# Gate projection in a decoder layer: five seven-product pairs between plain tiles, weight splits tied behind their place, and token sums over twelve steps

## The chip, the cores and the metric

The kernel runs on one core of one Trainium2 chip. The metric is the device time of one execution in microseconds; a run of the kernel before has a median of 2108.14 us over three runs (2105.8 to 2109.37).

Five engines work from their own queues: TensorE (PE in the profile, its weight loads PEld), VectorE (DVE), ScalarE (ACT), GpSimd (POOL) and SyncE (SP), which here issues the DMAs.

## What the kernel computes

One layer of a decoder on 1024 tokens of width 1024, in float32: a half-step SwiGLU, a mixing block, a half-step SwiGLU. The change lies in the mixing block. Its core in the reference:

```python
h = rms_norm(x, mix_norm)
q_lat, kv_lat, k_rope, fq, fk, fv, f_logit, g_mla, g_fox = split(h @ w_in)
y_mla = mla_mixer(...)   # 8 heads, causal softmax attention, 128-query blocks
y_fox = fox_mixer(...)   # 8 heads, the same with a cumulative log-forget-gate bias
mixed = (sigmoid(g_mla + b_gate[0]) * (y_mla @ w_branch_mla)
         + sigmoid(g_fox + b_gate[1]) * (y_fox @ w_branch_fox))
x = x + mixed @ w_o
```

`g_mla` and `g_fox` are each 1024 tokens by 1024 columns: the *gate projection*, `h` times 2048 columns of `w_in`. It needs nothing of the attention, and the attention needs nothing of it until the branches are mixed.

## The kernel before

**Products.** Every large product is made of float16 pairs: an operand is split into a high half (ScalarE: scale and cast, L167) and a low half (VectorE: scaled operand minus the high half, L170), both in `split_sb` (L161), and three matmuls (high-high, high-low, low-high) stand for one. A weight tile that comes by DMA goes through this split before TensorE can use it.

**Two ways to do the gate projection.** A *plain tile* (`gate_steps`, L1718) takes 128 columns: `col_load` brings them into a `stg` buffer, `col_split` makes `whi` and `wlo`, and each half of the tokens (512) takes 24 matmuls of 128x512 in two steps of 12. A *pair* (`gate_pairs`, L1753) takes 256 columns: the weight block and the token block are each cut in four quarters, and seven products of quarter sums give what eight products of quarters would (Strassen's scheme in Winograd's form). Each of the seven products is 12 matmuls and one step, so a pair takes 84 matmuls in 7 steps where two plain tiles take 96 in 8. For that it needs sums of the weight quarters and of the token quarters.

**Weight sums.** `operands` (L1062) makes them on GpSimd and is a Python generator. The sums `s3`, `a21+a22` and `s2` (L1068, L1069, L1070) come when a pair is begun; a fourth, the entry "-" of the order string, is `a12-s2` (L1075) and overwrites `a12`. Every further `next` splits one of the seven operands. The order is "12 11 - s2 s3 22 21 12": the first "12" is the untouched quarter, the last one the sum. `begin` (L1761) issues the load of a pair's weights into an `act` slot, `sums` (L1770) calls the generator for the three sums and the splits of "12" and "11", and `step` (L1780) does one product and draws the next operand. In steps q = 0 to 4 it draws one each: the "-" with `s2` in q = 0, then `s3`, 22, 21 and the last 12. At q = 4 the next pair's load is begun, at q = 6 its sums.

**Token sums.** `token_sums` (L889) forms four sums of token quarters on VectorE (L919 to L930), each in two halves, and splits them (high on ScalarE, L909; low on VectorE, L913): eight times a sum, a high and a low.

**The attention loop.** `attention` (L1847) runs 64 steps: 16 heads (8 MLA, then 8 FoX) of 4 steps, each step two 128-query blocks. A step does the scores of its two blocks (L1984), the row maximum on VectorE (`nm`, L1988), the exponential on ScalarE (L1991); then, one step late, the transposes of the probabilities on TensorE (L2010), their split (L167, L170), the product with the values (`pspv`, L2020 and L2025) and its combination (`cmb`: ScalarE L2027, VectorE L2028, GpSimd L2030 to L2032). After a pair of heads, `rest` (L2056) scales the result on GpSimd. Between these, gate steps are popped from a list so that TensorE has other matmuls while it waits for a softmax: 53 steps, about one a loop step, are dealt out over steps 0 to 53. Five plain steps are popped before the loop, 11 follow in steps 0 to 10, and the pairs come after them. The list `jobs` puts the parts of the forget-gate chain (`forget`, L1485) ahead of steps 0, 3, 5 and 6, the token sums ahead of steps 1 to 8 (a sum, a high and a low each), the first pair's load ahead of step 8 and its sums ahead of step 10. Near the end of the gate list, four `pieces` load and split the MLA attention result (`sta`, L2105) for the branch product, which starts at step 56.

**What sets the order.** The program is traced in this order, but a scheduler then sets each engine's queue by its own estimate of when an instruction becomes ready, so that an instruction can be placed ahead of others that were traced before it. On the chip each engine takes its queue in that fixed order. `follow(name)` (L147) adds an edge without a semaphore: the last traced instruction is placed behind the named one. `latest(engine)` (L191) is the last traced instruction of an engine. The splits of the weight sums have no such edge before the change.

**Buffers.** Tiles of one tag share a fixed number of slots: 8 of `u`, 4 each of `v`, `act` and `wd`. During the loop four `u` slots hold the split tokens and two the token sums; two `act` slots hold probabilities, one the values, and one is left for the weights of a pair.

Of the kernel before, what the change touches and what calls it, by code (L numbers as in the profile page):

```python
# [13 lines left out]
F16 = mybir.dt.float16  # L14
# [38 lines left out]
class Parts:  # L53
# [5 lines left out]
    def at(self, k, s=slice(None)):  # L59
        return self.tiles[k // self.per][:, k % self.per, s]  # L60
# [5 lines left out]
class Layer:  # L66
# [197 lines left out]
    def layer(self):  # L264
        src = self.i["x"][0]
# [49 lines left out]
        gates = []  # L315
        self.in_proj(hT, gates, lat["mark"])
        first = self.attention(gates, mix)
        ws = []
# [743 lines left out]
    def operands(self, w, scale, tags, order):  # L1062
# [10 lines left out]
        for name in order.split():  # L1073
            if name == "-":
                pool(out=a12, in0=a12, in1=s2, op=ALU.subtract)  # L1075
                self.behind = self.latest(mybir.EngineType.Pool)
                continue
            if tags is None:
                tag = ("stg", "whi", "wlo", "atp")[self.opn % 4]
                self.opn += 1  # L1080
            else:
                tag = next(tags)
            o = self.ring.tile([P, 2, 4, P], F16, tag=tag, bufs=2, name="op")
            self.split_sb(o[:, 0], o[:, 1], src[name], scale)
            yield o[:, 0], o[:, 1]
# [632 lines left out]
    def gate_steps(self, hT):  # L1718
# [3 lines left out]

        order = [(0, d, n) for d in range(4) for n in range(2)]
        weights = {}

        def prep(i):
            if i >= len(order):
                return
            s, d, n = order[i]
# [7 lines left out]
        def step(i, q):  # L1737
            s, d, n = order[i]
            if q == 0:
                self.gps = self.psb("psgate") if i % 2 and i < 2 else self.psg("psgate")  # L1740
                prep(i + 1)
            self.proj_half(self.gps, weights[i], hT, n, range(4 * q, 4 * q + 4))
# [6 lines left out]

        prep(0)  # L1750
        return [lambda a=(i, q): step(*a) for i in range(len(order)) for q in range(2)]

    def gate_pairs(self, every):  # L1753

        nc = self.nc
        w_in = self.i["w_in"][0]
        pairs = [(0, 4), (0, 6), (1, 0), (1, 2), (1, 4), (1, 6)]
        box = {"ops": []}
# [21 lines left out]
        def step(p, q):  # L1780
# [4 lines left out]
            e = box["e"]  # L1785
# [4 lines left out]
            self.product(ps, box["ops"].pop(0), every((1, 0, 3, 5, 6, 2, 4)[q]), first)  # L1790
            if q < 5:
                box["ops"].append(next(box["gen"]))

# [23 lines left out]
    def branch_mla_steps(self):  # L1817
# [4 lines left out]
        def piece(p):  # L1822
            if p == 0:
                box["at"] = [self.parts(tag, 4, 4, F16, 4096) for tag in ("u", "act")]
            self.split_at(box["at"], 0, p)
# [20 lines left out]

    def attention(self, gates, mix):  # L1847

# [27 lines left out]
        sum_of, high, low, every = self.token_sums(mix)  # L1876
        begin, sums, steps = self.gate_pairs(every)
        gates += steps
        total = len(gates)
        chain = self.forget()  # L1880
        jobs = {}
        at = lambda i, f: jobs.setdefault(i, []).append(f)
        for i in (0, 3, 5, 6):
            at(i, lambda: next(chain, None))
        for n, (k, e) in enumerate((k, e) for k in (3, 1, 2, 4) for e in range(2)):
            for f in (sum_of, high, low):
                at(n + 1, lambda f=f, k=k, e=e: f(k, e))
        at(8, lambda: begin(0))
        at(10, lambda: sums(0))
        for i in range(2 * HEADS * GR):  # L1890
# [18 lines left out]
            pr.append(self.scores(ops[k], 2 * g + 1, j, rs, pbuf))  # L1909
            if i <= 55:  # L1910
                while gates and done < total * (i + 1) / 55:
                    gates.pop(0)()
                    done += 1
                if len(gates) <= 3 and pieces:
                    pieces.pop(0)()
# [309 lines left out]
```

## Time and profile before

| | |
|---|---|
| median of 3 runs | 2108.14 us |
| the profiled execution | 2108.31 us, span of its instructions 2106.5 us |
| TensorE busy | 2040.2 us, 97% of the span |
| VectorE, ScalarE, GpSimd busy | 71%, 57%, 34% |
| attention with the gate steps, about 862 to 1335 us | TensorE busy 433.71 of 473 us, granted clock 0.96 |
| granted clock over the span | 0.989 |

All times in the profile are counted from the first instruction. A row of a group reads: line, engine, operation, tile written and tiles read, shape, count, then busy time and the mean of one in ns, then the engine's idle time just before such instructions and what ended it. In a table by stretches, each engine has its busy time and the count of instructions, and then come the granted TensorE clock (1.00 is full), the DMA engines' busy share and GB/s. A busy TensorE at a clock of 0.5 does half the work.

### The profile page before, as it was taken

Reading aid. Unit: us, or ns where it says so; the run is one execution under the profiler, and the core shown is the slowest. Engines: PE = TensorE matmul, PEld = TensorE weight load, DVE = VectorE, ACT = ScalarE, POOL = GpSimd, SP = SyncE. Lnnn points to the kernel's source line nnn. Section 1 sums busy time; section 2 is a strip of 40 time slices with the busy share of each in tenths; the row PEclk is TensorE's granted clock in tenths of the full one; section 3 lists DMA queues with packets and bytes.
Section 4 is the critical chain, followed back from the end, with each engine's and each line's share of the span. In section 5 each row is a group of like instructions: output and inputs, shape, how many; then the busy total and the mean of one; then the engine's idle time right before and its main releaser. Section 6 shows DMA issues by size and latency. Waiting matters only on the chain.

```text
span 2106.5 us, 28666 instructions
## 1 busy us (share of the span) xinstructions
PE 2040.2 (97%) x10175; PEld 1110.7 (53%) x10175; DVE 1504.6 (71%) x2515; ACT 1192.2 (57%) x2013; POOL 708.4 (34%) x759
## 2 busy tenths in 40 slices
PE   8999999999999999999998989999999999999999
PEld 5444444444447555466665655468544444444445
DVE  7856666788888788598777876864675555559876
ACT  6666665545555454477676765422556666555552
POOL 4455544752202121123332322000155554564300
PEclk9999999999999999999999999999999999999999
DMA  8258675675444564644454575452454464356433
GB/s 226 75 156 266 208 235 183 222 265 172 134 140 149 170 171 138 188 115 116 115 145 129 138 194 146 154 169 79 120 147 144 138 204 123 131 191 224 140 104 116
DMA packets 271546, 336.01 MB, mean 160 GB/s; under 512 B 21785, under 2 KB 201865, under 8 KB 271402
## 3 DMA queue, kind: packets, MB, share of 16 engines
q1 hardware_dynamic: 271402, 334.18, 52.1%
q8 instruction: 80, 1.31, 0.3%
q14 instruction: 64, 0.52, 0.1%
HBM read 240.32 MB, written 93.81 MB: 159 GB/s over the span
## 4 chain that ended last, share of the span: by engine, by line
PE 76%; DVE 11%; ACT 4%; DMA 3%; issue 3%; POOL 1%; SPq 1%; ACTq 0%; DVEq 0%; POOLq 0%
PE pst L1094 19%; PE psd L1247 15%; PE psb L1094 11%; PE psgate L1094 3%; PE psg L1094 3%; PE pspt L2010 3%; PE pss L1984 3%; DVE op L170 2%; PE pspv L2020 2%; PE psb L159 2%; PE psb L157 2%; PE psb L158 2%; PE psin L159 1%; PE psin L157 1%; PE psin L158 1%
## 5 line engine op out<-in xcount | busy, mean ns | idle before, releaser
L1094 PEld LDWEIGHTS <-op 128*128 128x128 f16 x3864 | 374.4, 98 | 439.9 <-issue 6.7
L1247 PE MATMUL psd<-op 128*128 128x512 f16 x1680 | 364.3, 379 | 1.8 <-DVE op L170 1.7
L1247 PEld LDWEIGHTS <-op 128*128 128x128 f16 x1680 | 164.3, 98 | 200.6 <-issue 3.5
L170 DVE SCALAR_TENSOR_TENSOR op<-s_u,s_v,op 128x512 f16<-128x512 f32 x170 | 151.0, 898 | 89.4 <-ACT op L167 88.8
L1094 PE MATMUL pst<-s_u,op 128*128 128x512 f16 x720 | 165.2, 379 | 1.3 <-DVE s_act L1142 1.3
L1094 PE MATMUL pst<-s_v,op 128*128 128x512 f16 x720 | 165.2, 379 | 1.3 <-DVE s_u L1142 1.3
L167 ACT ACTIVATE op<-s_u,s_v 128x512 f16<-128x512 f32 x170 | 118.0, 715 | 83.8 <-PE psd L1247 71.5
L170 DVE SCALAR_TENSOR_TENSOR op<-s_act,s_wd,op 128x512 f16<-128x512 f32 x130 | 117.8, 919 | 59.0 <-ACT op L167 59.0
L2010 PE MATMUL pspt<-ident,s_act 128*128 128x128 f32 x576 | 97.2, 290 | 30.7 <-ACT s_act L1991 17.5
L1991 ACT ACTIVATE s_act<-pss,nm 128x128 f32<-128x128 f32 (+7 forms) x128 | 94.4, 738 | 56.5 <-DVE nm L1988 55.6
L1984 PE MATMUL pss<-s_wd 96*128 96x256 f32 (+5 forms) x480 | 123.7, 381 | 0.7 <-DMA s_wd<-mk 0.6
L2030 POOL COPY atp<-cmb 64x128 f32<-64x128 f32 x64 | 24.3, 379 | 290.0 <-DVE cmb L2028 290.0
L1068 POOL TENSOR_TENSOR sums<-s_u 128x512 f32<-128x512 f32 x20 | 25.8, 1289 | 255.4 <-PE psa L615 160.9
L170 DVE SCALAR_TENSOR_TENSOR s_v<-pspt,s_v 128x512 f16<-128x512 f32 (+1 forms) x160 | 96.0, 630 | 13.8 <-ACT s_v L167 12.8
L2010 PEld LDWEIGHTS pspt<-ident,s_act 128*128 128x128 f32 x576 | 69.3, 147 | 61.3 <-ACT s_act L1991 34.1
L167 ACT ACTIVATE s_v<-pspt 128x512 f16<-128x512 f32 (+1 forms) x160 | 82.5, 552 | 24.9 <-PE pspt L2010 22.2
L1988 DVE TENSOR_REDUCE nm<-pss 128x1 f32<-128x128 f32 (+7 forms) x128 | 94.5, 750 | 1.6
L167 ACT ACTIVATE op<-s_wd 128x512 f16<-128x512 f32 x70 | 50.4, 721 | 78.6 <-PE psd L1247 74.9
L167 ACT ACTIVATE op<-s_act,s_wd 128x512 f16<-128x512 f32 x130 | 88.8, 710 | 6.6 <-PE pst L1094 4.1
L1094 PE MATMUL psgate<-s_u,op 128*128 128x512 f16 x360 | 87.8, 382 | 0.0
L1984 PEld LDWEIGHTS pss<-s_wd 96*128 96x128 f32 (+1 forms) x480 | 82.5, 201 | 8.9 <-ACT s_act L1991 0.9
L1094 PE MATMUL psb<-s_wd,op 128*128 128x512 f16 x360 | 82.6, 379 | 0.0
(566 smaller groups left out, 4575.0 us busy)
## 6 DMA issues: line engine op xcount, KB each, us to landing
sumd<-s_u SPq DMA_DIRECT2D x20, 1024.0 KB
s_u<-in_w_in_dram SPq DMA_DIRECT2D x19, 1024.0 KB
s_wd<-in_ffn_w_down_dram SPq DMA_DIRECT2D x32, 512.0 KB
sumd<-s_wd SPq DMA_DIRECT2D x13, 1024.0 KB
s_wd<-fd SPq DMA_DIRECT2D x48, 256.0 KB
s_act<-in_ffn_w_down_dram SPq DMA_DIRECT2D x22, 512.0 KB
s_wd<-sumd SPq DMA_DIRECT2D x14, 768.0 KB
s_u<-sumd SPq DMA_DIRECT2D x14, 768.0 KB
```

What stands on the lines that cost most here:

```text
L157: mm(out, lhsT=lh, rhs=rh, start=start, stop=False)
L158: mm(out, lhsT=lh, rhs=rl, start=False, stop=False)
L159: mm(out, lhsT=ll, rhs=rh, start=False, stop=stop)
L167: self.nc.scalar.activation(hi, src, AF.Copy, scale=scale)
L170: self.nc.vector.scalar_tensor_tensor(out=lo, in0=src, scalar=scale, in1=hi, op0=ALU.mult, op1=ALU.subtract)
L1094: mm(out, lhsT=a[:, k, :], rhs=b[:, k, :], start=start and k == 0 and i == 0, stop=k == n - 1 and i == 2, skip_group_check=True,)
L1247: nc.tensor.matmul(o, lhsT=u[:, r], rhs=w, start=start and m == 0, stop=k == CK - 1 and m == 2, skip_group_check=True,)
L1984: mm(ps[:, b:e], lhsT=a[:, q], rhs=bb[:, b:e], start=k == 0, stop=k == len(passes) - 1)
L1988: nc.vector.tensor_reduce(out=nm, in_=ps[:, :n], op=ALU.max, axis=AX.X, negate=True)
L1991: nc.scalar.activation(pn[:, :n], ps[:, :n], AF.Exp, bias=nm, accum_out=rs[:, i, j:j + 1])
L2010: nc.tensor.transpose(pt[:, o:o + P], pr[m][:, kt * P:(kt + 1) * P], self.ident)
L2020: mm(po[:, :256], lhsT=v[:, kt, :], rhs=slab[:, s, c, e * 256:(e + 1) * 256], start=kt == 0 and s == 0, stop=False,)
```

## The change

Plain tiles take six of the sixteen column blocks instead of four: (1, 0) and (1, 1) are added, so there are five pairs, without (1, 0). The order in the loop is 15 plain steps, 35 steps of pairs, then the last 4 plain steps, whose weights are loaded and split by a separate call (`behind`) in the last pair's step q = 5.

The operand generator now returns after the "-" too, and the pair's steps draw (1, 1, 2, 1, 1, 0, 0) times: the "-" alone at q = 0, `s2` at q = 1, `s3` and 22 at q = 2, 21 at q = 3, the last 12 at q = 4. Each split of a pair's operand is tied: its ScalarE half behind ScalarE's latest traced instruction, its VectorE half behind VectorE's.

The token sums, highs and lows are a list of 24, taken two a step in steps 1 to 12, after the step's scores instead of ahead of the step; highs and lows are tied as the splits are. The first pair's load comes in step 11 and its sums in step 13. The forget chain's parts move to steps 2, 4, 6 and 8. Both halves of the MLA branch operand lie in `u` slots, and the `pieces` start with four gate steps left instead of three.

```diff
@@ operands
             if name == "-":
                 pool(out=a12, in0=a12, in1=s2, op=ALU.subtract)
                 self.behind = self.latest(mybir.EngineType.Pool)
+                if tags is not None:
+                    yield None
                 continue
...
-            self.split_sb(o[:, 0], o[:, 1], src[name], scale)
+            last = ()
+            if tags is not None:
+                last = self.latest(mybir.EngineType.Activation), self.latest(mybir.EngineType.DVE)
+            self.split_sb(o[:, 0], o[:, 1], src[name], scale, last)
             yield o[:, 0], o[:, 1]
@@ gate_steps
-        order = [(0, d, n) for d in range(4) for n in range(2)]
+        order = [(s, d, n) for s, d in ((0, 0), (0, 1), (0, 2), (0, 3), (1, 0), (1, 1)) for n in range(2)]
...
-                prep(i + 1)
+                if i + 1 not in (10, 12):
+                    prep(i + 1)
...
-        return [lambda a=(i, q): step(*a) for i in range(len(order)) for q in range(2)]
+        return [lambda a=(i, q): step(*a) for i in range(len(order)) for q in range(2)], lambda: prep(10)
@@ gate_pairs
-        pairs = [(0, 4), (0, 6), (1, 0), (1, 2), (1, 4), (1, 6)]
+        pairs = [(0, 4), (0, 6), (1, 2), (1, 4), (1, 6)]
...
-            if q < 5:
-                box["ops"].append(next(box["gen"]))
+            for _ in range((1, 1, 2, 1, 1, 0, 0)[q]):
+                o = next(box["gen"])
+                if o is not None:
+                    box["ops"].append(o)
+            if (p, q) == (len(pairs) - 1, 5):
+                behind()
@@ branch_mla_steps
-                box["at"] = [self.parts(tag, 4, 4, F16, 4096) for tag in ("u", "act")]
+                box["at"] = [self.parts(tag, 4, 4, F16, 4096) for tag in ("u", "u")]
@@ attention
-        gates += steps
+        gates[15:15] = steps
...
-        for i in (0, 3, 5, 6):
+        for i in (2, 4, 6, 8):
             at(i, lambda: next(chain, None))
-        for n, (k, e) in enumerate((k, e) for k in (3, 1, 2, 4) for e in range(2)):
-            for f in (sum_of, high, low):
-                at(n + 1, lambda f=f, k=k, e=e: f(k, e))
-        at(8, lambda: begin(0))
-        at(10, lambda: sums(0))
+        pinned = []
+        for k, e in ((k, e) for k in (3, 1, 2, 4) for e in range(2)):
+            for f, engine in ((sum_of, None), (high, mybir.EngineType.Activation), (low, mybir.EngineType.DVE)):
+                pinned.append((engine, lambda f=f, k=k, e=e: f(k, e)))
...
             if i <= 55:
+                for engine, f in pinned[2 * i - 2:2 * i] if i else ():
+                    last = engine and self.latest(engine)
+                    f()
+                    if last:
+                        self.follow(last)
+                if i == 11:
+                    begin(0)
+                if i == 13:
+                    sums(0)
...
-                if len(gates) <= 3 and pieces:
+                if len(gates) <= 4 and pieces:
```

More of the change, by code (lines that the diff above doesn't have):

```diff
@@ L316, in layer @@
         self.in_proj(hT, gates, lat["mark"])
-        first = self.attention(gates, mix)
+        first = self.attention(*gates, mix)
         ws = []
@@ L1721, in gate_steps @@
         w_in = self.i["w_in"][0]
-        order = [(0, d, n) for d in range(4) for n in range(2)]
+        order = [(s, d, n) for s, d in ((0, 0), (0, 1), (0, 2), (0, 3), (1, 0), (1, 1)) for n in range(2)]
         weights = {}
         def prep(i):
-            if i >= len(order):
-                return
             s, d, n = order[i]
@@ L1750, in gate_steps, with gate_pairs @@
         prep(0)
-        return [lambda a=(i, q): step(*a) for i in range(len(order)) for q in range(2)]
-    def gate_pairs(self, every):
+        return [lambda a=(i, q): step(*a) for i in range(len(order)) for q in range(2)], lambda: prep(10)
+    def gate_pairs(self, every, behind):
         nc = self.nc
         w_in = self.i["w_in"][0]
-        pairs = [(0, 4), (0, 6), (1, 0), (1, 2), (1, 4), (1, 6)]
+        pairs = [(0, 4), (0, 6), (1, 2), (1, 4), (1, 6)]
         box = {"ops": []}
@@ L1844, in branch_mla_steps, with attention @@
         return pieces, lambda: prep(0), gates, [lambda last=False, a=(d, n): step(*a, last) for d in range(KD) for n in range(2)]
-    def attention(self, gates, mix):
+    def attention(self, gates, more, mix):
         nc = self.nc
@@ L1876, in attention @@
         sum_of, high, low, every = self.token_sums(mix)
-        begin, sums, steps = self.gate_pairs(every)
-        gates += steps
+        begin, sums, steps = self.gate_pairs(every, more)
+        gates[15:15] = steps
         total = len(gates)
```

## The prediction

> **What bounds the kernel now.** I read the page first, then the waits of the stretch in which the gate pairs run, then the timelines around its holes, then a table by stretches.
>
> ```profile
> span 2106.5 us, 28666 instructions
> PE 2040.2 (97%) x10175; PEld 1110.7 (53%) x10175; DVE 1504.6 (71%) x2515; ACT 1192.2 (57%) x2013; POOL 708.4 (34%) x759
> ...
> PE 76%; DVE 11%; ACT 4%; DMA 3%; issue 3%; POOL 1%; SPq 1%; ACTq 0%; DVEq 0%; POOLq 0%
> ```
>
> TensorE is busy for 97% of the span and carries 76% of the chain that ended last. So only two things count: matmuls added or removed, and holes of TensorE, with the slow clock that follows a hole. The profiled execution took 2108.31 us, 1.8 more than its span and 0.17 more than the median of 2108.14; I work from 2108.3.
>
> The waits between 950 and 1250 us, TensorE's first, then two of ScalarE's:
>
> ```profile
> PE pspt L2010 <- DVE cmb L2028: 10.8, 6, 4.0
> PE pspt L2010 <- ACT s_act L1991: 9.3, 10, 3.3
> ```
>
> ```profile
> ACT op L167 <- POOL sums L1070: 13.1, 5, 4.0
> ACT op L167 <- POOL sums L1068: 2.4, 1, 2.4
> ```
>
> (us in total, times, longest.) TensorE waits for softmax results, 20.1 us in all. ScalarE, which makes them, stands 15.5 us in front of a weight-sum split whose sum GpSimd has not finished. Both come together around 1183 us, on ScalarE, then GpSimd, then TensorE:
>
> ```profile
> 1185.10 0.72 ACT L167 ACTIVATE op<-sums,ws 128x512 f16<-128x512 f32 x1 [4.01 <-POOL sums L1070]
> 1185.85 0.58 ACT L2027 COPY cmb<-pspv 64x512 f32<-64x512 f32 x1
> 1186.45 1.11 ACT L1991 ACTIVATE s_act<-pss,nm 128x1024 f32<-128x1024 f32 x1
> ```
>
> ```profile
> 1180.80 1.26 POOL L1068 TENSOR_TENSOR sums<-s_act 128x512 f32<-128x512 f32 x1
> ...
> 1183.81 1.26 POOL L1070 TENSOR_TENSOR sums<-s_act 128x512 f32<-128x512 f32 x1
> ```
>
> ```profile
> 1187.27 0.33 PE L2010 MATMUL pspt<-ident,s_act 128*128 128x128 f32 x1 [4.04 <-DVE cmb L2028]
> ```
>
> ScalarE is idle for 4.01 us until the third sum ends (1183.81 + 1.26 = 1185.07). Behind the blocked split stand the `cmb` copy and an exponential, and TensorE, out of other work, is idle for 4.04 us. The split was put into the queue too early: the scheduler thought the sum would be there.
>
> The table by stretches gives the size of each hole. After its length, a row's first figure is TensorE's busy time; the granted clock stands third from the end.
>
> ```profile
> 886.00:894.00 8.00, 6.02 (x18) 3.53 (x17) 3.28 (x9) 4.56 (x11) 1.13 (x6) 0.59 0.88 206
> 919.00:953.00 34.00, 31.43 (x189) 20.30 (x188) 32.69 (x52) 24.38 (x48) 10.94 (x15) 1.00 0.50 123
> 956.00:968.00 12.00, 8.97 (x53) 5.83 (x51) 11.80 (x15) 7.17 (x13) 6.71 (x7) 1.00 0.46 135
> 1004.00:1010.00 6.00, 5.04 (x31) 3.50 (x29) 5.08 (x9) 4.48 (x10) 3.07 (x4) 1.00 0.78 220
> 1040.00:1050.00 10.00, 8.26 (x39) 6.01 (x38) 6.75 (x10) 7.01 (x13) 3.52 (x5) 0.83 0.04 4
> 1050.00:1116.00 66.00, 65.32 (x406) 44.58 (x405) 50.16 (x95) 49.66 (x102) 20.35 (x37) 1.00 0.60 156
> 1120.00:1132.00 12.00, 9.47 (x60) 5.95 (x58) 9.58 (x15) 8.55 (x18) 3.28 (x7) 1.00 0.82 211
> 1142.00:1156.00 14.00, 10.70 (x47) 6.94 (x46) 9.33 (x16) 7.34 (x13) 6.68 (x8) 0.76 0.18 57
> 1182.00:1194.00 12.00, 7.96 (x46) 5.76 (x44) 6.87 (x13) 6.57 (x13) 5.98 (x7) 0.86 0.60 146
> 1236.00:1246.00 10.00, 7.74 (x50) 4.88 (x49) 7.19 (x14) 6.74 (x14) 1.75 (x5) 1.00 0.95 204
> 1250.00:1282.00 32.00, 22.48 (x115) 16.77 (x113) 23.32 (x40) 19.42 (x40) 5.12 (x14) 0.79 0.80 232
> ```
>
> Five of these stretches (956, 1004, 1040, 1142 and 1182) hold a pair's sums on GpSimd. Their idle time of TensorE is 3.03 + 0.96 + 1.74 + 3.30 + 4.04 = 13.07 us. The one pair left of the six has its sums inside 1050:1116, where none of ScalarE's splits had to wait long for them: 0.68 us of idle in 66 us.
>
> **The change part by part.**
>
> *Splits behind GpSimd and tied.* `s2` was drawn in the step after its pair's sums; now the step after that, and no split may be placed ahead of its traced place. From 962.6 to 1247.2 us there are 42 products:
>
> ```profile
> L1094 PE MATMUL psgate<-s_u,op x360: 376/379/634, 962.6 to 1247.2; 128*128 128x512 f16 x180
> ```
>
> That is 6.8 us a step, so a split two steps behind the sums has some 13 us, and GpSimd's chain took 4.3 us above (1180.80 to 1185.07). The five holes should close. With them goes the slow clock: (1 - 0.83) x 10 + (1 - 0.76) x 14 + (1 - 0.86) x 12 = 6.7 us; some of a hole may itself lie in a slow stretch, so I count 5.7. Together 18.8 us. Bounds: nothing if other waits refill the holes, 19.8 if all goes. Since that one pair was free of it already and showed almost no idle time, I take 85%: -16.0.
>
> [...]
>
> *Five pairs instead of six.* Two plain tiles take 8 steps, a pair 7, so one step of 12 matmuls is added. The chain shows such a step back to back:
>
> ```profile
> 983.12 2.61 PE psgate L1094 x12
> ```
>
> It lies on TensorE's own path: +2.6. What goes, seven splits on ScalarE and VectorE and four sums on GpSimd, lies beside TensorE and is counted at nothing. Its cover is that TensorE has matmuls all through 1050:1116 while VectorE is busy for 50 and ScalarE for 50 of 66 us; less work there cannot lengthen it.
>
> *Two more plain tiles.* Each needs a load, one `whi` and one `wlo`, queued without a tie. These rows, between 862 and 1335 us, tell what such tiles made TensorE wait:
>
> ```profile
> L157 PE MATMUL psgate<-s_u,whi 128*128 128x512 f16 x64 | 25.1, 392 | 4.0 <-ACT z L1747 2.8 <-ACT whi L167 1.1
> L159 PE MATMUL psgate<-s_u,wlo 128*128 128x512 f16 x64 | 24.9, 388 | 1.6 <-DVE wlo L170 1.6
> ```
>
> The `whi` and `wlo` waits are 2.7 us for all tiles prepared in that time. Two more cost between 0 and 2.7 us; I take +1.8, since the last tile's load joins a queue that the 1236 stretch shows busy (DMA share 0.95).
>
> *Token sums over twelve steps.* In 919:953 VectorE is busy for 32.69 of 34 us and TensorE idle for 2.57: VectorE is the limit there. A third of the work moves four steps on, which is worth up to -2.6. But part of the sums was placed before the attention:
>
> ```profile
> 814.41 1.22 DVE L919 TENSOR_TENSOR t<-s_u 128x1024 f32<-128x1024 f32 x1
> ...
> 824.11 1.22 DVE L926 TENSOR_TENSOR s_u<-s_u 128x1024 f32<-128x1024 f32 x1
> ```
>
> Those are the first and the last of six such instructions, 7.3 us of VectorE, and the tied lows among them come back into the loop. If all came out on TensorE it would be +7; as they spread over twelve steps I take 0, between -2.6 and +3.
>
> *Forget chain from step 2.* ScalarE at the loop's start:
>
> ```profile
> 881.92 1.28 ACT L1504 ACT_TABLE_LOAD   x1
> ...
> 885.87 1.28 ACT L1747 ACT_TABLE_LOAD   x1 [2.39 <-PE pss L1984]
> 887.16 0.78 ACT L1747 ACTIVATE z<-psgate,bg,ws 128x512 f32<-128x512 f32 x1
> ```
>
> The chain's logarithm (L1504) comes with a table load, and the next `z` with another, which holds it up; TensorE loses 1.98 us in 886:894, then 3.3 to the clock. The reload moves with the chain to step 2 and will hold up something there. From -4 to +2; I take -1.
>
> *What the ties cost.* A split used to fill a gap of ScalarE wherever it was ready; now it stands behind its step's second exponential and ahead of the `cmb` copy. Were each of the 35 to hold that copy for 0.72 us (the split's time above) on TensorE's path, that would be 25 us. The 1050 row speaks against it, as ScalarE and VectorE are each a quarter idle there; nearer to that end, +2.
>
> *Other holes.* 1120:1132 has 2.53 us, 1236:1246 2.26 and 1250:1282 9.5. The last comes after the gate steps are used up, which they are at the same step as before. The second belongs to the pieces' loads, which still share SP's queue with the heads' operands and with the write of the scaled result. For the first, where splits crowd on VectorE, I take half: -1.2. The `u` slot in place of `act` and the pieces a step earlier only move loads: 0.
>
> Sum: -16.0 + 2.6 + 1.8 + 0 - 1 + 2 - 1.2 = -11.8, so 2108.3 - 11.8 = 2096.5 us. With the ends of the single terms the likeliest case runs from 2091 to 2102.
>
> **The rivals.**
>
> *More goes than forecast.* All 18.8 us, the 2.6 of VectorE's stretch, the 2.5 of 1120:1132 and the 1 at the start, with 2.6 us of matmuls and nothing new: -22.3, 2086 us. For it speaks the smooth 66 us, against it that every engine's queue is new.
>
> *The holes re-form.* Only half of the 16.0 goes, because ScalarE then waits for something else (a token sum by VectorE, a `psgate` result): -3.8, 2104.5 us. Against it: none of these waits in 950 to 1250 us is as long as GpSimd's.
>
> *Slower: the load takes the sums' place.* One `act` slot is free, so a pair's load starts when the last 12 of the pair before is split. Untied, that split ran early; tied, it comes in step q = 4, some 5 us into it, and the next pair's first splits stand tied in step q = 6, ahead of an exponential. Two steps are 13.6 us, so the load has about 11. On SP's queue and on GpSimd:
>
> ```profile
> 1069.78 1.02 SPq L1768 DMA_DIRECT2D s_act<-in_w_in_dram  x2
> ```
>
> ```profile
> 1075.83 1.62 POOL L1068 TENSOR_TENSOR sums<-s_act 128x512 f32<-128x512 f32 x1 [1.96 <-issue]
> ```
>
> Issued at 1069.78, used at 1075.83: 6 us when nothing is ahead. If a head's operands go first and the load takes over 11 us, ScalarE blocks as it does now. At the price of the 1182 row (4.04 + 1.7) four pairs cost 22.9: -11.8 + 22.9 = +11, 2119 us. [...]
>
> [...]
>
> **How the numbers follow.** Forecast 0.58, more goes 0.13, clock rule 0.05, holes re-form 0.12, slower 0.12. A measurement of this kernel can tell about 0.2%, 4.2 us, from no change. Faster by more: 0.58 + 0.13 + 0.05 = 0.76; within: 0.12; slower by more: 0.12. The range from 2086 to 2108 holds the first four and leaves out the slower case and the tails.
>
> **What would show it.** ScalarE's wait for GpSimd's sums falls from 15.5 us to under 3, TensorE's two waits at L2010 between the first and the last product from 20.1 to under 9, and the clock stays at 1.00 from the first to the last product; `psgate` has 12 matmuls more (696 becomes 708). It would be wrong if ScalarE's splits wait for `s_act<-in_w_in_dram` by more than 3 us each, if VectorE or ScalarE waits at a tied high or low of the token sums and opens holes of TensorE in steps 1 to 12, or if 1250:1282 grows.

## The result, and the profile after

The changed kernel has a median of 2076.97 us (2076.17 to 2077.89, four runs) against 2108.76 for the kernel before on the same chip: ratio 0.9852, 95% interval 0.9835 to 0.9869. That is 31.8 us, where 11.8 were forecast; the time lies below the range. Repeated later on another chip (run e0), the ratio was 0.9869 (0.9854 to 0.9884). The forecast had the direction, and a third to a half of the size. One execution of run a2 below took 4221.86 us, and its median and ratio are those of the other three.

The page of the kernel after, three lines:

```profile
span 2076.1 us, 28667 instructions
PE 2029.6 (98%) x10187; PEld 1101.2 (53%) x10187; DVE 1495.3 (72%) x2507; ACT 1186.2 (57%) x2005; POOL 696.9 (34%) x755
...
PE 77%; DVE 11%; ACT 5%; DMA 3%; issue 3%; SPq 0%; POOL 0%; ACTq 0%; DVEq 0%; POOLq 0%
```

TensorE has the 12 matmuls more (10175, now 10187) and is busy for 10.6 us less: busy time also counts the stretches of slow clock (gate matmuls in a row start 216 ns apart in the trace of before, by the median, and 427 where the granted clock was 0.50, by six such gaps; the longest gate matmul took 650 ns before and 392 after, the median one 379 in both). To see where the span went I cut both traces at the row maximum that opens loop steps 0, 12, 42, 54 and 60. The table by stretches, of the kernel before:

```profile
886.30:969.90 83.60, 75.92 (x441) 50.33 (x440) 72.34 (x113) 56.55 (x111) 27.97 (x40) 0.96 0.51 129
969.90:1170.80 200.90, 189.54 (x1135) 128.34 (x1135) 150.42 (x271) 140.79 (x288) 64.03 (x110) 0.97 0.50 127
1170.80:1251.00 80.20, 72.94 (x441) 48.28 (x440) 61.53 (x108) 56.59 (x114) 26.42 (x45) 0.98 0.60 154
1251.00:1300.40 49.40, 40.01 (x210) 26.58 (x208) 35.34 (x58) 27.38 (x52) 10.56 (x21) 0.86 0.68 197
```

And of the kernel after, the same loop steps:

```profile
884.10:963.40 79.30, 73.87 (x444) 49.50 (x443) 67.83 (x120) 55.79 (x109) 17.44 (x39) 1.00 0.53 137
963.40:1152.40 189.00, 185.73 (x1139) 124.56 (x1140) 147.18 (x269) 138.91 (x286) 63.48 (x109) 1.00 0.50 130
1152.40:1231.00 78.60, 73.28 (x448) 47.35 (x445) 64.34 (x110) 57.47 (x116) 25.19 (x45) 1.00 0.65 175
1231.00:1270.90 39.90, 35.70 (x207) 23.54 (x206) 33.82 (x56) 25.60 (x50) 10.40 (x21) 0.96 0.75 216
```

Read each row as length, TensorE's busy time, and the clock at the end. Steps 0 to 11 lost 4.3 us, steps 12 to 41 lost 11.9, steps 42 to 53 lost 1.6, and steps 54 to 59, which have no gate step at all, lost 9.5; the rest of the program changed by 3.1 us, so the span by 30.4. From step 12 to 53 TensorE's idle time fell from 18.6 to 8.6 us and its clock is 1.00, as forecast. The 9.5 us behind the gate steps were forecast at nothing. Beside the prediction's terms: steps 12 to 53 lost 13.5 us where -16.0 + 2.6 + 1.8 + 2 - 1.2 = -10.8 was forecast, steps 0 to 11 lost 4.3 where 1 was, and steps 54 to 59 hold the largest part of the miss.

The waits of the kernel after, between 950 and 1235 us (us in total, times, longest), ScalarE's first:

```profile
ACT s_act L2007 <- DVE nm L2004: 41.8, 35, 2.1
ACT s_v L167 <- PE pspt L2026: 8.9, 16, 2.5
```

```profile
PE pspt L2026 <- ACT s_act L2007: 5.6, 10, 1.7
PE pspt L2026 <- DVE cmb L2044: 2.1, 2, 1.9
```

ScalarE no longer waits for GpSimd's sums at all (15.5 us before); TensorE's wait for softmax results fell from 20.1 to 7.7 us. What is left on ScalarE is chiefly the wait for VectorE's row maximum, 41.8 us here and 36.8 before.

### The profile page after: what moved, and what is told of

Its sections match the earlier page's. It is cut to its first block, busy times and chain, and to the rows that moved or that the text cites. A ratio compares the mean times of both kernels' runs of the same rounds, so it can differ in the third digit from the quotient of the medians.

```text
span 2076.1 us, 28667 instructions
## 1 busy us (share of the span) xinstructions
PE 2029.6 (98%) x10187; PEld 1101.2 (53%) x10187; DVE 1495.3 (72%) x2507; ACT 1186.2 (57%) x2005; POOL 696.9 (34%) x755
## 4 chain that ended last, share of the span: by engine, by line
PE 77%; DVE 11%; ACT 5%; DMA 3%; issue 3%; SPq 0%; POOL 0%; ACTq 0%; DVEq 0%; POOLq 0%
PE pst L1099 19%; PE psd L1252 16%; PE psb L1099 11%; PE psg L1099 3%; PE pss L2000 3%; PE pspt L2026 3%; PE psgate L1099 3%; DVE op L170 2%; PE psb L159 2%; PE psb L157 2%; PE psb L158 2%; PE pspv L2036 2%; ACT s_act L2007 2%; PE psin L159 1%; PE psin L157 1%
## 5 line engine op out<-in xcount | busy, mean ns | idle before, releaser
L1099 PEld LDWEIGHTS <-op 128*128 128x128 f16 x3780 | 366.1, 98 | 434.3 <-issue 4.9
L1252 PEld LDWEIGHTS <-op 128*128 128x128 f16 x1680 | 164.4, 98 | 200.5 <-issue 3.4
L2000 PE MATMUL pss<-s_wd 96*128 96x256 f32 (+5 forms) x480 | 118.9, 367 | 2.5 <-ACT s_act L2007 1.9
L2046 POOL COPY atp<-cmb 64x128 f32<-64x128 f32 x64 | 18.7, 292 | 292.5 <-DVE cmb L2044 292.3
L2000 PEld LDWEIGHTS pss<-s_wd 96*128 96x128 f32 (+1 forms) x480 | 78.1, 192 | 10.2 <-ACT s_act L2007 3.5
L1099 PE MATMUL psb<-s_u,op 128*128 128x512 f16 x360 | 82.6, 379 | 0.0
```

The source lines that it names most:

```text
L1099: mm(out, lhsT=a[:, k, :], rhs=b[:, k, :], start=start and k == 0 and i == 0, stop=k == n - 1 and i == 2, skip_group_check=True,)
L1252: nc.tensor.matmul(o, lhsT=u[:, r], rhs=w, start=start and m == 0, stop=k == CK - 1 and m == 2, skip_group_check=True,)
L2000: mm(ps[:, b:e], lhsT=a[:, q], rhs=bb[:, b:e], start=k == 0, stop=k == len(passes) - 1)
```

## The experiments

"Worth" below is (1 - ratio) times 2104 us, close to the middle one of the kernel before's medians beside these runs (2103.43 to 2106.93); each ratio is to the kernel before on the same chip, with its 95% interval. A table by stretches shows one execution: the same code in the same queue order took 79.3 us for steps 0 to 11 in one and 82.3 in another (the kernel after and a4), so a difference of a few us between two tables needs the ratios beside it. The first theory was that of the prediction: the ties close GpSimd's holes, and the pair that goes is worth nothing. The rivals: the pair that goes, or what stands behind the gate steps, carries the rest.

**The splits alone** (b3: the kernel before, with the changed `operands` and draws).

```diff
+                if tags is not None:
+                    yield None
                 continue
...
+            last = ()
+            if tags is not None:
+                last = self.latest(mybir.EngineType.Activation), self.latest(mybir.EngineType.DVE)
-            self.split_sb(o[:, 0], o[:, 1], src[name], scale)
+            self.split_sb(o[:, 0], o[:, 1], src[name], scale, last)
...
-            if q < 5:
-                box["ops"].append(next(box["gen"]))
+            for _ in range((1, 1, 2, 1, 1, 0, 0)[q]):
+                o = next(box["gen"])
+                if o is not None:
+                    box["ops"].append(o)
```

> The kernel before with the new draws and the ties of the pairs' splits alone, six pairs behind eleven plain steps. Theory one: ScalarE's wait for GpSimd's sums falls from 15.5 us to under 3, and the steps with pairs shorten by 12 to 18 us; if that is all it does, 2090 to 2096, with steps 54 to 59 as long as before (49.5 us). If the ties also bring the branch products forward, these steps shorten by 8 to 10 us and the time is 2081 to 2087.

Measured: 2089.0 us, 0.9927 (0.9907 to 0.9947), worth 15.4 us. The terms of the prediction that belong to it (-16.0, +2 for the ties, -1.2) make -15.2. ScalarE has no wait for GpSimd's sums left, and TensorE's two waits are 7.1 and 3.3 us. Its table by stretches, steps 12 to 41, 42 to 53 and 54 to 59:

```profile
971.60:1161.20 189.60, 183.30 (x1117) 122.42 (x1116) 147.22 (x269) 136.88 (x283) 63.46 (x106) 1.00 0.52 135
1161.20:1235.70 74.50, 70.36 (x430) 45.54 (x429) 61.18 (x109) 56.44 (x116) 24.89 (x42) 1.00 0.61 159
1235.70:1281.50 45.80, 38.53 (x214) 25.00 (x213) 37.88 (x58) 27.49 (x52) 10.56 (x22) 0.93 0.71 207
```

200.9 became 189.6, and 80.2 became 74.5: 17.0 us of the gain lie within the gate steps, where it was forecast. But 49.4 became 45.8 as well, behind them, so the splits are not quite alone in the 15.4; why is shown below, under what stands behind the gate steps.

**Which part of it** (a1: the change without the ties; a2: with the ties, but `s2` drawn at q = 0 again).

```diff
 a1
-            if tags is not None:
-                last = self.latest(mybir.EngineType.Activation), self.latest(mybir.EngineType.DVE)
 a2
-            for _ in range((1, 1, 2, 1, 1, 0, 0)[q]):
+            for _ in range((2, 1, 1, 1, 1, 0, 0)[q]):
```

> The changed kernel without the ties of the pairs' splits (the draws, the five pairs, the token sums and the rest stay). Theory one: the ties keep ScalarE from standing in front of a sum that GpSimd has not finished, so without them ScalarE waits for GpSimd's sums by 8 us or more again between the first and the last product, and the time rises by 6 to 14 us, to 2083 to 2091. Theory two: drawing s2 a step later is enough; then ScalarE's wait stays under 3 us and the time within 4 us of 2077.

> The changed kernel with the draws of before (s2 at q = 0, s3, 22, 21 and the last 12 after it), ties kept. Theory one (the ties do it): 2077 to 2081, since a tied s2 stands in its own step, where GpSimd needs about 4 us. Theory two (the later draw does it): ScalarE waits for GpSimd's sums again, four or five times by 1 to 4 us, 2083 to 2091.

a1: 2083.21 us, 0.9901 (0.9881 to 0.9921). a2: 2074.67 us, 0.9857 (0.9834 to 0.9881), not told apart from the change. The waits of ScalarE in a1 between 940 and 1260 us hold the old line again (6.4 us, under the 8 expected), and steps 12 to 27 of its table by stretches show the cost:

```profile
ACT op L167 <- POOL sums L1070: 6.4, 3, 5.0
```

```profile
963.90:1078.20 114.30, 105.61 (x620) 71.52 (x618) 85.16 (x145) 75.74 (x154) 41.27 (x62) 0.96 0.45 115
```

The changed kernel takes 103.0 us for these sixteen steps. a2 has no such wait. So the tie keeps the split behind its place; with the tie, the later draw isn't needed.

**Five pairs alone** (e1: the kernel before, with plain tiles for (1, 0) and (1, 1), in the order 11 plain steps, 35 of pairs, 8 plain; splits, token sums, chain and pieces as before), and **five pairs with the splits** (e2: e1 with b3's edit).

```diff
-        order = [(0, d, n) for d in range(4) for n in range(2)]
+        order = [(s, d, n) for s, d in ((0, 0), (0, 1), (0, 2), (0, 3), (1, 0), (1, 1)) for n in range(2)]
...
-        pairs = [(0, 4), (0, 6), (1, 0), (1, 2), (1, 4), (1, 6)]
+        pairs = [(0, 4), (0, 6), (1, 2), (1, 4), (1, 6)]
...
-        gates += steps
+        gates[11:11] = steps
```

> The kernel before with five pairs in place of six and nothing else: 11 plain steps, 35 of pairs, 8 plain, the first pair's load and sums at steps 8 and 10 as before; splits untied and drawn as before. By the prediction's terms (12 matmuls more, two plain tiles more) it is 2 to 5 us slower than before: ratio 1.001 to 1.002. Theory six: the last pair's hole at 1182 (5.7 us) goes with the pair, and the branch weights' load comes ahead of the last head's operands on SP's queue (5 to 9 us): ratio 0.993 to 0.996.

> As the run before, with the changed draws and ties of the pairs' splits. Theory six: splits alone gave 0.9927; with five pairs the branch weights' load adds 3 to 6 us to that, and 8 plain steps at the end instead of a pair's splits some more: 0.987 to 0.990. By the prediction's terms: 0.993 to 0.995.

e1: 2084.34 us, 0.9905 (0.9890 to 0.9920), worth 20.0 us, where the prediction's terms for it say +4.4; it is more than theory six expected, too. e2: 2075.56 us, 0.9864 (0.9849 to 0.9879), worth 28.6: beside e0's 0.9869 on the same chip, these two edits give as much as the whole change. They overlap: 15.4 + 20.0 is 6.8 more than both together give, though the three intervals leave that sum open by some 6 us. Where e1 gains is plain in its table by stretches (steps 12 to 41, 42 to 53, 54 to 59):

```profile
967.70:1166.50 198.80, 191.07 (x1154) 128.14 (x1154) 150.57 (x274) 141.75 (x290) 65.72 (x112) 0.99 0.52 131
1166.50:1238.20 71.70, 70.90 (x436) 45.98 (x434) 56.70 (x100) 52.33 (x105) 20.24 (x38) 1.00 0.68 187
1238.20:1276.10 37.90, 34.01 (x198) 22.62 (x197) 31.11 (x54) 23.78 (x47) 8.73 (x20) 0.95 0.74 210
```

Among the pair steps (the first row) almost nothing changes, as the splits are still untied and ScalarE still waits 8.9 us for `sums`. Steps 42 to 53 fall from 80.2 to 71.7 us, TensorE's idle time in them from 7.26 to 0.80: the plain tiles now stand where the last pair's hole was, and VectorE and ScalarE have 4.8 and 4.3 us less to do. Steps 54 to 59 fall from 49.4 to 37.9. With the splits tied, the steps where the last pair stood hardly gain any more: steps 42 to 53 take 74.5 us in b3 and 73.7 in e2, while steps 54 to 59 fall from 45.8 to 34.5.

**What stands behind the gate steps.** The loads of the first branch weights and of the last heads' operands, on SP's queue of the kernel before, and TensorE around them:

```profile
1259.48 3.74 SPq L1968 DMA_DIRECT2D s_wd<-fd  x6
...
1264.19 0.95 SPq L655 DMA_DIRECT2D stg<-in_w_branch_mla_dram  x2
```

```profile
1265.00 1.20 PE L2010 MATMUL pspt<-ident,s_act 128*128 128x128 f32 x9 [2.23 <-ACT s_act L1991]
1271.81 0.55 PE L2010 MATMUL pspt<-ident,s_act 128*128 128x128 f32 x3 [1.20 <-ACT s_act L1991]
...
1275.79 0.88 PE L2010 MATMUL pspt<-ident,s_act 128*128 128x128 f32 x6 [1.53 <-ACT s_act L1991]
1280.63 0.38 PE L157 MATMUL psg<-s_u,whi 128*128 128x512 f16 x1
```

And after:

```profile
1228.65 1.00 SPq L655 DMA_DIRECT2D stg<-in_w_branch_mla_dram  x2
...
1237.98 3.65 SPq L1984 DMA_DIRECT2D s_wd<-fd  x6
```

```profile
1238.18 0.48 PE L157 MATMUL psg<-s_u,whi 128*128 128x512 f16 x1
```

Before, the branch weights are issued behind the last heads' operands, the first branch product (`psg`) starts 29.6 us into the stretch, and until then TensorE has nothing to put between one exponential and the next. After, the weights go first and the product starts 7.2 us in; the same waits are then filled with branch matmuls. Three runs test that order. d1 is the kernel before with the branch preparation called in step 54; d2 is the changed kernel with the branch load tied behind the operand loads; d3 is the changed kernel with branch steps allowed from step 54 on.

```diff
 d1
+                if i == 54:
+                    prep()
...
-                    prep()
                     sig()
 d2 (col_load)
             nc.sync.dma_start(st[:, k0:k0 + nk, :], src)
+            if self.hold:
+                self.follow(self.hold)
...
+                    self.hold = self.latest(mybir.EngineType.SP)
                     prep()
+                    self.hold = None
 d3
-            if i <= 55:
+            if i <= 53:
...
-                if i == 55 + 1:
+                if i == 54:
```

> The kernel before with one move: the first branch weights are prepared in step 54 instead of step 56, so that their load stands on SP's queue ahead of the last head's operand loads instead of behind them. Theory four: that order alone is why steps 54 to 59 took 49.5 us before and 39.9 after; then they take 42 to 46 us, the first branch product comes about 10 us after the start of step 54 (29.7 before), and the time falls by 4 to 8 us, ratio 0.996 to 0.998. Rival: the stretch is bound by the softmax alone and the order is beside the point; then ratio 0.999 to 1.001.

> The changed kernel with the first branch weights' load tied behind the last head's operand loads on SP's queue, as it stood before. Theory four: the first branch product moves from 7 to some 20 to 28 us after the start of step 54, steps 54 to 59 become 5 to 10 us longer, 2082 to 2087. Rival: within 3 us of 2077.

> The changed kernel with the branch products begun two steps earlier, at step 54, where the gate steps have run out and nothing fills the softmax's waits (2.3 us of idle time in step 54). If filling them there is worth something: 2072 to 2075. If the branch's weights and gates come too late for it: 2077 or a little above.

d1: 2099.41 us, 0.9977 (0.9965 to 0.9989), worth 4.8 us; its load is issued ahead (1255.01 against 1259.19) and the stretch falls from 49.4 to 42.4:

```profile
1250.70:1293.10 42.40, 35.33 (x200) 23.88 (x198) 34.08 (x56) 26.12 (x49) 8.62 (x19) 0.92 0.75 222
```

d2: 2081.95 us, 0.9895 (0.9878 to 0.9912), by the ratios 5 to 9 us slower than the change's two; its first branch product starts 25.8 us in. Its steps 54 to 59 are short, with 177 matmuls to 207, since branch matmuls move past step 60, so the row to compare is that from step 54 to the end of attention, of the change and then of d2:

```profile
1231.00:1302.80 71.80, 67.49 (x400) 43.83 (x399) 60.46 (x101) 44.65 (x86) 15.05 (x33) 0.98 0.54 159
```

```profile
1233.40:1308.80 75.40, 67.03 (x394) 43.60 (x393) 59.94 (x100) 44.77 (x86) 15.97 (x33) 0.98 0.51 151
```

That is 3.6 us; another 3.1 of this execution lie in steps 0 to 11, whose code d2 doesn't touch. So the order on SP's queue is worth 4.8 us in the kernel before (2.3 to 7.4 by the interval) and, by the rows, nearer to 4 in the change. d3: 2080.28 us, 0.9885 (0.9866 to 0.9903): starting the branch steps earlier as well gains nothing.

The number of pairs isn't what turns this order. With six pairs and tied splits the load stands ahead too; in b3:

```profile
1240.83 1.09 SPq L655 DMA_DIRECT2D stg<-in_w_branch_mla_dram  x2
1243.03 3.01 SPq L1975 DMA_DIRECT2D s_wd<-fd  x5
```

Its first branch product starts 10.9 us into step 54, where it was 29.6 before. The load also stands ahead in c1, with six pairs, and in every other run here but d2, which forces it back. So the splits and the five pairs each turn the order when made alone, and together can gain it only once, which would account for most of the overlap of 6.8 us.

**The early load and the splits, with six pairs** (f2: b3 with d1's edit).

> The kernel before with six pairs, with the changed draws and ties, and with the first branch weights prepared in step 54. The splits alone gave 0.9927, the early load alone 0.9977. If the two add up and nothing else is wrong with six pairs: 0.989 to 0.991. If the sixth pair's steps themselves are what is dear, it stays at 0.992 to 0.993, against 0.9864 with five pairs and the same splits.

Measured: 2085.42 us, 0.9897 (0.9878 to 0.9916), worth 21.7 us; 15.4 + 4.8 = 20.2. The number fits the sum, but the run doesn't test it: b3 has the load ahead already, all 790 DMA issues stand in the same order in b3 and f2, and the first branch product starts 10.9 us into step 54 in both. The intervals of b3 and f2 overlap. Against e2, 7 us (2 to 12) are left that six pairs still cost. Steps 54 to 59 of f2, then of e2:

```profile
1238.40:1280.00 41.60, 35.87 (x211) 22.81 (x209) 35.91 (x57) 27.18 (x53) 9.70 (x22) 1.00 0.76 222
```

```profile
1236.30:1270.80 34.50, 32.33 (x200) 21.44 (x198) 29.52 (x52) 22.57 (x46) 9.55 (x21) 1.00 0.72 193
```

7.1 us lie here, 3.5 of busy and 3.6 of idle TensorE. VectorE has 6.4 us more to do in f2's stretch and ScalarE 4.6: with six pairs, more of their work runs on into it. The load's place is not the same in the two, either: e2 issues it 23.9 us ahead of step 54 and f2 5.1 us behind its start. Which of the two counts, and why instructions move, was not tried.

**The number and the place of the pairs.** c1: the change with six pairs (11 plain steps, 42 of pairs). d4: the change with 11, 35 and 8. a3: with 19 and 35, no plain tile last. e3: e2 with 15, 35 and 4. f1: the change with four pairs (15, 28 and 12). The lines that follow from these (the list of plain tiles, the steps of the first pair's load and sums) are left out here.

```diff
 c1
-        pairs = [(0, 4), (0, 6), (1, 2), (1, 4), (1, 6)]
+        pairs = [(0, 4), (0, 6), (1, 0), (1, 2), (1, 4), (1, 6)]
...
-        gates[15:15] = steps
+        gates += steps
...
 d4
-        gates[15:15] = steps
+        gates[11:11] = steps
...
 a3
-        gates[15:15] = steps
+        gates += steps
...
 e3 (against e2)
-        gates[11:11] = steps
+        gates[15:15] = steps
...
 f1
...
-        pairs = [(0, 4), (0, 6), (1, 2), (1, 4), (1, 6)]
+        pairs = [(0, 4), (0, 6), (1, 4), (1, 6)]
```

> The changed kernel with six pairs again, behind eleven plain steps and with none after them, the first pair's load at step 7 and its sums at step 9; ties, draws, token sums over twelve steps, chain and branch slots stay. One step of 12 matmuls less is -2.6 us. If the number of pairs has no other effect: 2074 to 2076 from the changed kernel, or 2078 to 2080 by the run with the pairs last. If five pairs are what brings the branch weights' load forward, steps 54 to 59 become 8 to 10 us longer: 2083 to 2088.

> The changed kernel with the five pairs four steps earlier, as they began before: 11 plain steps, 35 of pairs, 8 plain, the first pair's load at step 7 and its sums at step 9, in the middle of the token sums. Theory five: VectorE is the bound in steps 0 to 12, and taking the first pair's splits out of them is part of the gain; then steps 0 to 12 become 3 to 6 us longer and the time 2080 to 2084. Rival: only the number of pairs counts; then within 3 us of 2077.

> The changed kernel with the four plain steps moved ahead of the pairs: 19 plain steps, then 35 of pairs, load and sums of the first pair four steps later. Theory three: the gain behind the gate steps (steps 54 to 59, 9.6 us of span) comes from plain tiles being last, since the pieces' loads and the branch weights' loads no longer stand on SP's queue behind the last pair's store; then 2084 to 2088, and the branch products again begin only about step 59. Rival: the slots and the earlier pieces do it; then within 3 us of 2077.

> As the run before, with 15 plain steps ahead of the pairs and 4 behind, the first pair's load and sums at steps 12 and 14, behind the token sums, which stay as before (steps 1 to 8, untied). Theory five (VectorE is the bound in steps 0 to 12, and the first pair's splits among the token sums cost 3 to 5 us there): 0.985 to 0.988, as the changed kernel. If it needs the token sums over twelve steps as well: as the run before.

> The changed kernel with four pairs instead of five: 15 plain steps, 28 of pairs, 12 plain. If fewer pairs are a gain in themselves, because VectorE and ScalarE have less to do: 2072 to 2075, though TensorE has 12 matmuls (2.6 us) more. If five pairs gained by what the sixth pair's place had cost (its hole, and the branch weights' load behind it): 2078 to 2081, the matmuls' price and the pair's.

c1: 2091.86 us, 0.9938 (0.9919 to 0.9956). d4: 2081.38 us, 0.9891 (0.9873 to 0.9909). They differ by the sixth pair and two plain tiles at the end: about 10 us. c1 lies above all that was expected of it: its load is ahead and its steps 54 to 59 take 41.3 us, so that neither theory there explains it. a3: 2081.02 us, 0.9891 (0.9868 to 0.9913). e3: 2082.21 us, 0.9890 (0.9873 to 0.9906). By their intervals a3, d4 and e3 can't be told from one another; by the middle ratios they stand 4 to 8 us behind the change, and e3 5.5 behind e2, so the place of the pairs counts as well. Theory three is out: a3 has pairs last and its first branch product still starts 10.1 us into step 54. Theory five came in d4 (VectorE as the bound of the first steps: steps 0 to 11 take 84.3 us instead of 79.3) and missed in e3 (0.985 to 0.988 expected), whose steps 54 to 59 take 42.9 us to e2's 34.5. f1: 2074.04 us, 0.9848 (0.9834 to 0.9863), the lowest of all, but too near to the change's own two ratios (0.9852 and 0.9869) to be told apart from both. It computes 12 matmuls more than the change, and steps 42 to 53 take 73.9 us instead of 78.6:

```profile
1152.50:1226.40 73.90, 72.16 (x445) 47.67 (x444) 58.74 (x104) 54.70 (x108) 20.93 (x41) 1.00 0.76 208
```

VectorE has 5.6 us less work in it and TensorE is idle for 1.74 us instead of 5.32. So it isn't shown that the saved matmuls of a fifth pair pay for its splits and sums.

**The small edits.** a4: the change with the second half of the branch operand in `act` again and the pieces from three steps left. b1: with the token sums in steps 1 to 8, untied. b2: with the chain in steps 0, 3, 5 and 6.

```diff
 a4
-                box["at"] = [self.parts(tag, 4, 4, F16, 4096) for tag in ("u", "u")]
+                box["at"] = [self.parts(tag, 4, 4, F16, 4096) for tag in ("u", "act")]
...
-                if len(gates) <= 4 and pieces:
+                if len(gates) <= 3 and pieces:
 b1
...
+        for n, (k, e) in enumerate((k, e) for k in (3, 1, 2, 4) for e in range(2)):
+            for f in (sum_of, high, low):
+                at(n + 1, lambda f=f, k=k, e=e: f(k, e))
 b2
-        for i in (2, 4, 6, 8):
+        for i in (0, 3, 5, 6):
```

> The changed kernel with the branch operand's halves in u and act again and the pieces started with three gate steps left. Theory three (plain tiles last): within 3 us of 2077. Rival (slot and pieces): 2084 to 2088, with the branch products beginning about step 59.

> The changed kernel with the token sums as before: a sum, a high and a low ahead of each of steps 1 to 8, untied. If spreading and tying them is what shortened steps 0 to 11 by 4.3 us of span, those steps become 3 to 5 us longer, 2080 to 2083. If the moved forget chain did it, within 2 us of 2077.

> The changed kernel with the forget chain's parts at steps 0, 3, 5 and 6 as before. If the chain's table loads at the loop's start made the hole and the slow clock at 886 to 894 us, both return: up to step 2 some 3 to 5 us are lost, 2080 to 2083. If the token sums did it, within 2 us of 2077.

a4: 2078.13 us, 0.9877 (0.9857 to 0.9898). b1: 2079.69 us, 0.9888 (0.9868 to 0.9908). b2: 2075.97 us, 0.9868 (0.9846 to 0.9890). None is told apart from the change. In e1 these three stand as in the kernel before, and its branch weights are still issued early (1235.87, the operands at 1245.41): the slots and the pieces aren't needed to move them.

> The changed kernel as it is, once more beside the three that follow, so that all four stand against the same runs of the kernel before. Ratio 0.984 to 0.987.

e0, the change once more beside e1 to e3: 2076.94 us, 0.9869 (0.9854 to 0.9884).

## Why the prediction was wrong

**Splits behind GpSimd and tied, -16.0, with the ties' +2 and the -1.2.** Right in mechanism: -15.2 said, -15.4 measured in b3, of which the gate steps alone show 17.0. All its signs came in the changed kernel: ScalarE's wait for GpSimd 15.5 to 0, TensorE's 20.1 to 7.7, the clock 1.00. The reason given was half right: the tie does it, the later draw is not needed (a1, a2). Sizing it at 85% of the holes' idle time and lost clock, by the one pair that had none, was a sound reading. That the two totals differ by 0.2 is luck: b3 also brings the branch load ahead, which the terms don't hold, and its profile is longer than that of before by 3.9 us outside steps 12 to 59.

**Five pairs instead of six, +2.6, and two more plain tiles, +1.8.** This step failed: +4.4 said, -20.0 measured with the old splits (e1). What goes was "counted at nothing", and "less work there cannot lengthen it" looked at 1050:1116, the smoothest stretch, and generalized it. By its place, what goes is the last pair. With the old splits go the hole at 1182, 4.04 us of idle that the splits' term also counts, and 4.8 us of VectorE's and 4.3 of ScalarE's work in steps 42 to 53, where both feed TensorE's transposes. Within the gate steps, and with the splits tied, the terms were not far off: steps 12 to 53 take 264.1 us in b3, 265.7 in e2 and 267.6 in the change. What the terms miss is the effect behind the gate steps: steps 54 to 59 take 45.8 us in b3, 34.5 in e2 and 39.9 in the change.

**Other holes: 1250:1282, 0.** The same failure from the other side, and the largest part of the miss: 0 said, 9.5 us measured over steps 54 to 59. "The last comes after the gate steps are used up, which they are at the same step as before" is true and beside the point. The hole was 9.5 us long in part because the branch weights came late, and they came late by their place on SP's queue, which an edit further up shifted. That order is worth 4.8 us by itself (d1). Where the rest of the 9.5 comes from stays open: the load comes earlier still in the change than in d1, and VectorE and ScalarE have less to do in the stretch, but no run parts the two. The queue's two rows were in the trace of before.

**Token sums 0, forget chain -1.** Not refuted: b1 and b2 differ from the change by less than a run can tell. The tied highs and lows opened no large hole: TensorE is idle for 5.4 us in steps 0 to 11, 7.7 before.

**The rivals.** "The load takes the sums' place" did not come: no wait of ScalarE for `s_act<-in_w_in_dram` is in the waits after. The wait for a pair's load moved to GpSimd, 4.9 us once, and held up no split. "The holes re-form" is out by b3 (worth 11.2 to 19.6 us; half of the term would leave some 7). The chances give 0.05 to a clock rule that no run shows: before, the clock fell to 0.83 over ten microseconds with 1.74 us of idle and to 0.76 over fourteen with 3.30, and in b3 it is 1.00 in steps 12 to 53. "More goes" (2086) had the right sign and stopped at the holes of the gate steps, as did the range.

**What stays open.** Why the scheduler puts the branch load behind the operands in the kernel before alone; and what exactly moves 7 us in steps 54 to 59 between f2 and e2. Both gains are measured, their causes are not. Of the 30.4 us, the 4.3 of steps 0 to 11 are not settled either: a4, with the same code and the same order of all queues there, takes 82.3 us where the change takes 79.3, at a clock of 0.96 instead of 1.00, so part of it comes and goes with the clock.

## What to carry to other kernels

A scheme that saves matmuls by extra sums and splits has to be priced on the engines that feed TensorE, at the place where it stands: here the sixth pair saved 2.6 us of matmuls, and with the branch load ahead in both, kernels without it were 7 and 10 us faster (e2 to f2, d4 to c1). From b3 to e2 the gain lay behind the pair's own steps, so the steps that follow belong to the price. When an edit adds or removes loads or slots, read the order of the DMA queue behind the edit, in steps that it does not touch, since the next phase's first load may change places. Where a split of an operand can block an engine's queue in front of the softmax, tie it to its traced place; that took away 17 us of the steps in which it stands. In the kernel before, a row maximum ended at 1183.74, and its exponential started only at 1186.45, behind a split for which ScalarE had been idle for 4.01 us.

## What the runs showed of the hardware

The largest hole left between steps 42 and 53 is no wait for GpSimd's result, but VectorE beside GpSimd. The timeline of the kernel after:

```profile
1159.59 3.50 DVE L170 SCALAR_TENSOR_TENSOR op<-s_act,ws,op 128x512 f16<-128x512 f32 x2
...
1160.04 2.50 POOL L2072 TENSOR_TENSOR atp<-atp,rb 128x1024 f32<-128x1024 f32 x1 [1.00 <-DMA rb<-rd]
...
1163.01 0.67 DVE L2044 TENSOR_TENSOR cmb<-pspv,cmb 64x512 f32<-64x512 f32 x1
...
1163.74 0.55 PE L2026 MATMUL pspt<-ident,s_act 128*128 128x128 f32 x3 [1.89 <-DVE cmb L2044]
```

The group of these splits (shortest, median and longest in ns) shows how far that is from the usual:

```profile
L170 DVE SCALAR_TENSOR_TENSOR op<-s_act,ws,op x25: 739/748/2840, 975.8 to 1193.4; 128x512 f16<-128x512 f32 x25
```

Two splits of some 0.75 us took 3.50 together beside a GpSimd product of 2.50 us, the `cmb` behind them came late, and TensorE was idle for 1.89 us. In the kernel before one split took 2.70 us at 1118.84 beside the same product (2.39 us, from 1118.60). In both places the split started while the product ran, alone or as the second of two, and ended 0.55 us behind it. So do the others: in the two traces, 202 splits of an `op` tile of this shape start while a GpSimd tensor-tensor instruction has more than 0.4 us left, and 201 of them end 0.54 or 0.55 us behind it; the median one of the group above takes 0.75. What makes the split wait is not shown.

The clock: a hole of 1.89 us, and 5.3 us of idle in 78.6, left it at 1.00 in the changed kernel, where the kernel before showed 0.83 over ten microseconds with 1.74 us idle. The idle time of a stretch doesn't decide it: up to 1207 us, a4 runs the changed kernel's instructions in the same order on every queue, and the clock falls in a4 alone. Between 904 and 920 us, the changed kernel and then a4:

```profile
904.00:912.00 8.00, 4.76 (x25) 2.56 (x23) 5.33 (x18) 6.29 (x12) 2.08 (x9) 1.00 0.63 150
912.00:920.00 8.00, 7.51 (x52) 5.39 (x53) 7.04 (x12) 4.72 (x10) 1.13 (x4) 1.00 0.03 4
```

```profile
904.00:912.00 8.00, 4.29 (x23) 2.47 (x22) 4.65 (x16) 5.62 (x11) 2.43 (x10) 0.95 0.59 140
912.00:920.00 8.00, 8.00 (x38) 5.38 (x39) 5.73 (x9) 3.18 (x6) 0.00 (x0) 0.63 0.00 0
```

TensorE is idle for 3.73 us in the one and 3.71 in the other. In the trace of before, the seven falls between 862 and 1335 us last 3.41 or 6.83 us and start whole multiples of 3.41 us apart, and in the 3.41 us ahead of each TensorE was idle for 47 to 83%. Whether the place of a hole against that beat counts is not shown: the changed kernel's hole of 1.89 us made 55% of one such period, and the clock held. What decides when the clock falls is not settled here.
